# A ConvFFN's down-projection by seven products of half blocks in place of eight, in a two-layer decoder step on one core

## The chip, the core and the metric

The kernel runs on one core of a Trainium2 chip. The metric is the device time of one launch in microseconds (us). The core has a matrix engine (TensorE, PE in the profile; PEld is its loading of weights), a vector engine (VectorE, DVE), a scalar engine (ScalarE, ACT), GpSimd (POOL) and SyncE (SP), which here issues nearly all DMA. Each engine executes its own instructions in order; between engines, semaphores decide.

## What is computed

Two decoder layers over 1024 prompt tokens and 8 x 8 sample tokens, 1088 columns in all (`T`), in float32. Each layer has attention and a gated mixer, and then a gated ConvFFN with 1024 model and 2816 hidden channels:

```python
def _layer(x, c, pos, attend, conv_prev, p):
    ...
    x = x + g_a * (jnp.concatenate([a_out, s_out], axis=-1) @ p['w_out'])
    h = _rmsnorm(x, p['g_ffn']) * (1 + sc_f) + sh_f
    hu = h @ p['w_ffn_in']
    ext = jnp.concatenate([conv_prev.astype(hu.dtype), hu], axis=1)
    conv = p['conv_b'] + sum(p['conv_w'][j] * ext[:, j:j + t] for j in range(CONV_W))
    gate, up = jnp.split(conv, 2, axis=-1)
    x = x + g_f * ((jax.nn.silu(gate) * up) @ p['w_ffn_out'])
    return x, k, v, vg, ext[:, -(CONV_W - 1):]
```

The last product, `silu(gate) * up` by `w_ffn_out` (2816 x 1024), is the down-projection. The scales and shifts (`sh`, `sc`, `g`) come from a conditioning vector by a product with `w_ada`. Outputs are the activations, the key and convolution caches and the gate rows.

## The kernel before

Activations lie transposed: 128 channels on the partitions, the 1088 columns along a row. Every factor of a matmul is split by `split` into a high part (ACT copies it into a shorter float type) and a low part (DVE subtracts that from the original), and a product is three matmuls: high by high, high by low, low by high (`mm3`, lines 304 to 306 of the profile).

A layer runs through these stages, each with its pools of SBUF and PSUM:

- Attention, mixer and output projection. Between its pieces stand calls of `ada`, each 4 matmuls of a 256-column piece of `w_ada`, which make the scales that later stages need; layer 0 has 32 of them left to do, layer 1 has 48.
- **First phase**, the up-projection with convolution and gate. It loops over 22 blocks `f` of 128 hidden channels for the gate and 128 for the up half. The product of the weights by `h` is cut into blocks (two halves of channels by two halves of 544 columns, `HT`) and done by seven products in place of eight, with sums of weights (`diff`, 128x512 on DVE) and of activations. Its matmuls are `prod` (line 918) into the accumulators X, Y, Z, of 272 columns (`HC`) each. PE works through f while DVE and ACT do the convolution of f before (`conv`, lines 949 to 956) and the gate (`gate`, line 960); the result is written to DRAM as `pd[f]` by a DMA of POOL. `tail` closes the last f.
- **Second phase**, the down-projection. `down(g)` runs for six groups: three thirds of the columns (384, 384, 320) by two halves `mh` of the 1024 outputs. A group has four accumulators `y` of one PSUM bank, and loops over all 22 f: `half_unit` loads a 128x512 piece of weights (`ro`) and splits it into `oh` and `ol`, `load_prod` loads a third of `pd[f]` (`pr`) and splits it into `ph` (for the first half only, it is kept for the second), and then come 12 matmuls. The weights are thus loaded and split three times. After a group, `residual` adds its outputs to `xs`, and they go to DRAM. In layer 0 `hook` puts the next layer's norm of a third (squares on ACT, sums on POOL and PE in `nrma`, broadcast by PE in `nrba`, products on DVE) into the groups 2 and 4, and 16 calls of `ada` into the groups 1 and 3. The norm of the last third, and after it the next layer's first products `zv` in `zv_all`, follow the down-projection.

The order of work on an engine is set by the program's scheduler from the order of the code and the free buffers of the pools.

## Time and profile before

| | |
|---|---|
| runs | 2318.65, 2320.19, 2322.41 us; median 2320.19 |
| profiled execution | 2321.23 us, span 2319.4 us |
| busy share | PE 97%, PEld 92%, DVE 67%, ACT 47%, POOL 12% |
| chain that ended last | PE 89%, DVE 5%, DMA 2%, ACT 2%, issue 1%, POOL 1% |
| layer 0: first phase, down-projection | 431.45 to 901.3, 904.28 to 1191.6 us |
| layer 1: first phase, down-projection | 1577.9 to 2044.4, 2051.68 to 2315.1 us |

The span runs from the first to the last instruction; the execution's own time is 1.8 us longer. The chain is followed back from the last instruction to what released each step. The clock granted to PE is 1.00 at full speed. PE's matmuls overlap, so that the spacing of their starts, or their count in a stretch, tells their price and not the length of one. What stands behind "<-" in brackets names what ended an engine's idle time.

### The profile page before, as it was taken

The numbers are of one execution on the slowest core, as the hardware profiler recorded it, in microseconds if no ns is written. First come the engines' busy times: TensorE is split into PE (matmuls) and PEld (weight loads), VectorE is DVE, ScalarE is ACT, GpSimd is POOL, SyncE is SP. The second block draws the span as 40 slices with busy tenths as digits, with TensorE's granted clock in tenths as the row PEclk, the third lists the DMA queues.
The fourth block names the chain that finished last, engine by engine and source line by source line (L and its number), as shares of the span: only waits on it lengthen the run. The fifth ranks groups of instructions, "written<-read, shape, count | busy, mean of one in ns | idle before, by whom it ended". The sixth has DMA issues, their size and how long they took to land.

```text
span 2319.4 us, 41013 instructions
## 1 busy us (share of the span) xinstructions
PE 2258.1 (97%) x15838; PEld 2129.6 (92%) x15838; DVE 1559.5 (67%) x3400; ACT 1087.7 (47%) x2110; POOL 286.5 (12%) x426
## 2 busy tenths in 40 slices
PE   7999999999999999999999999999999999989999
PEld 5898789899999999999988987898999999989999
DVE  5837854887777776464758378369777777764544
ACT  5524533644545445353544255246544544453443
POOL 1000002132111211000000000112211121100000
PEclk9999999999999999999999999999999999999999
DMA  9220244322222224767651002641222222156665
GB/s 354 100 91 1 68 154 161 132 87 77 81 80 79 78 73 155 245 207 236 204 179 61 32 1 77 236 166 47 83 80 77 83 79 78 63 188 196 222 208 169
DMA packets 138116, 289.02 MB, mean 125 GB/s; under 512 B 22400, under 2 KB 63680, under 8 KB 137920
## 3 DMA queue, kind: packets, MB, share of 16 engines
q1 hardware_dynamic: 130176, 261.08, 34.4%
q0 software_dynamic: 7744, 25.33, 2.8%
q8 instruction: 124, 2.03, 0.4%
q14 instruction: 72, 0.59, 0.1%
HBM read 242.54 MB, written 43.80 MB: 123 GB/s over the span
## 4 chain that ended last, share of the span: by engine, by line
PE 89%; DVE 5%; DMA 2%; ACT 2%; issue 1%; POOL 1%; SPq 0%; DVEq 0%; ACTq 0%; POOLq 0%
PE X L918 22%; PE Y L918 11%; PE o L313 7%; PE y L304 7%; PE y L305 7%; PE y L306 7%; PE Z L918 6%; PE zu L313 4%; PE s L644 2%; PE ada L130 1%; PE av L732 1%; PE zv L306 1%; PE q L304 1%; PE zv L305 1%; PE zv L304 1%; PE q L305 1%
## 5 line engine op out<-in xcount | busy, mean ns | idle before, releaser
L304 PE MATMUL y<-ph,oh 128*128 128x384 f32 (+1 forms) x1056 | 347.4, 330 | 10.8 <-ACT ph L181 10.8
L305 PE MATMUL y<-ph,oh 128*128 128x384 f32 (+1 forms) x1056 | 347.0, 329 | 2.4 <-DVE ph L182 2.4
L306 PE MATMUL y<-ph,ol 128*128 128x384 f32 (+1 forms) x1056 | 346.0, 328 | 0.0
L182 DVE TENSOR_TENSOR ol<-ro,oh 128x512 fp32r<-128x512 f32 x264 | 183.1, 698 | 189.5 <-ACT oh L181 172.7
L181 ACT ACTIVATE oh<-ro 128x512 fp32r<-128x512 f32 x264 | 165.5, 628 | 216.9 <-PE y L305 106.2
L951 DVE SCALAR_TENSOR_TENSOR cv<-hu,lc,cv 128x1023 f32<-128x1023 f32 (+1 forms) x168 | 215.1, 1280 | 59.1 <-ACT cv L949 59.1
L304 PEld LDWEIGHTS y<-ph,oh 128*128 128x128 f32 x1056 | 199.2, 189 | 18.1 <-ACT ph L181 11.5
L305 PEld LDWEIGHTS y<-ph,oh 128*128 128x128 f32 x1056 | 199.9, 189 | 3.7 <-DVE ph L182 3.7
L306 PEld LDWEIGHTS y<-ph,ol 128*128 128x128 f32 x1056 | 199.8, 189 | 0.0
L941 POOL COPY hus<-halo 128x16 f32<-128x16 f32 x88 | 85.2, 969 | 366.6 <-issue 258.8
L313 PE MATMUL o<-hhm,wh 128*128 128x384 f32 (+1 forms) x384 | 120.8, 334 | 0.0
L313 PE MATMUL o<-hhm,wl 128*128 128x384 f32 (+1 forms) x384 | 119.1, 329 | 0.3 <-DVE wl L164 0.3
L313 PE MATMUL o<-hlm,wh 128*128 128x384 f32 (+1 forms) x384 | 118.7, 329 | 0.4 <-DVE hlm L182 0.4
L949 ACT ACTIVATE cv<-hu,lc 128x1088 f32<-128x1088 f32 x84 | 108.5, 1291 | 19.3 <-DVE hu L1017 19.3
L182 DVE TENSOR_TENSOR ph<-pr,ph 128x384 fp32r<-128x384 f32 (+1 forms) x132 | 72.2, 551 | 50.9 <-ACT ph L181 50.1
L181 ACT ACTIVATE ph<-pr 128x384 fp32r<-128x384 f32 (+1 forms) x132 | 66.1, 503 | 70.6 <-DMA pr<-pd 68.9
L163 ACT ACTIVATE wh<-r 128x1024 fp32r<-128x1024 f32 x44 | 46.3, 1056 | 91.5 <-PE zu L313 64.8
L164 DVE TENSOR_TENSOR wl<-r,wh 128x1024 fp32r<-128x1024 f32 x40 | 48.9, 1223 | 55.6 <-ACT wh L163 45.7
L313 PEld LDWEIGHTS o<-hhm,wh 128*128 128x128 f32 x384 | 71.7, 189 | 6.6 <-issue 4.9
L956 ACT ACTIVATE cv<-cv 128x1088 f32<-128x1088 f32 x42 | 46.8, 1114 | 64.8 <-DVE cv L953 64.8
L313 PEld LDWEIGHTS o<-hhm,wl 128*128 128x128 f32 x384 | 71.7, 189 | 2.2 <-issue 1.6
L313 PEld LDWEIGHTS o<-hlm,wh 128*128 128x128 f32 x384 | 71.8, 189 | 2.1 <-DVE hlm L182 1.0
(400 smaller groups left out, 6258.9 us busy)
## 6 DMA issues: line engine op xcount, KB each, us to landing
r<-in_w SPq DMA_DIRECT2D x132, 512.0 KB, 3.5
ro<-in_w SPq DMA_DIRECT2D x264, 256.0 KB, 3.3
ra<-in_w_ada SPq DMA_DIRECT2D x64, 512.0 KB, 4.7
pd<-cv POOLq DMA_DIRECT2D x42, 544.0 KB, 3.0
pr<-pd SPq DMA_DIRECT2D x88, 192.0 KB, 3.6
rb<-in_w_ada SPq DMA_DIRECT2D x16, 512.0 KB, 7.7
ra<-in_w_ada SPq DMA_DIRECT2D x32, 256.0 KB, 4.2
pr<-pd SPq DMA_DIRECT2D x44, 160.0 KB, 3.6
```

The lines of the kernel that those rows point to most:

```text
L164: eng.tensor_tensor(out=wl, in0=raw, in1=wh.bitcast(F32), op=ALU.subtract)
L181: r = nc.scalar.activation(out=h, in_=x, func=AF.Copy)
L182: eng.tensor_tensor(out=lo, in0=x, in1=h.bitcast(F32), op=ALU.subtract)
L304: r = nc.tensor.matmul(pt, lhsT=lh, rhs=rh, start=first, stop=False)
L305: nc.tensor.matmul(pt, lhsT=lh, rhs=rl, start=False, stop=False)
L306: nc.tensor.matmul(pt, lhsT=ll, rhs=rh, start=False, stop=last)
L313: nc.tensor.matmul(pts[t][:, :n], lhsT=lhsT, rhs=r[t][:, k, :], start=f, stop=e)
L918: nc.tensor.matmul(pt[:, i, :HC], lhsT=a[:, k * P:(k + 1) * P], rhs=b[:, k, i * HC:(i + 1) * HC], start=(first and k == 0 and a is wh and ...
L941: nc.gpsimd.tensor_copy(rs[:, :, :2], halos[f][:, i])
L949: nc.scalar.activation(out=a, in_=hu, func=AF.Identity, scale=w2, bias=cb)
L951: nc.vector.scalar_tensor_tensor(out=a[:, sh:NP], in0=hu[:, :NP - sh], scalar=wt, in1=a[:, sh:NP], op0=ALU.mult, op1=ALU.add)
L956: nc.scalar.activation(out=a, in_=a, func=AF.Silu)
```

## The change

The product of the second phase is done as the first phase's is. With the weights cut into halves of hidden channels (blocks i and i + 11 of the 22) by halves of outputs, and the activations into the same halves of hidden channels by halves of columns (544), the eight products of half blocks become seven, some of sums of blocks:

- The sums of activations are formed in the first phase: f now runs in pairs (i and i + 11, list `F`), and after each second one `gate` does four additions or subtractions of 128x544 on DVE (the last in `last_sum`, after the next product), and four DMAs write seven blocks, `pd[i]`, of 544 columns, where two wrote two whole ones.
- The sums of weights are formed in the second phase by DVE, 128x512 each: `t1`, `t4` (both kept in SBUF for a later product), `t2` and `t3`.
- Products follow in the order A11, A12, S2, S3, A22, S1 and S4, each of 11 steps i with 4 accumulators of two PSUM banks and 24 matmuls of 272 columns (`mm_pairs`, line 1149 after). S4 is run in two halves of the outputs. Between products DVE adds the accumulators to kept sums (`plus`), ACT copies those of the first (`r1`), and `res_early` and `res_late` add finished quarters to `xs`. The pool "pc" has four tiles of two banks; that leaves no bank free.
- Loads: weights come in as 128x1024, 128x512 or 128x256 pieces, activations as 128x544.
- The next layer's norm: the last third inside the second half of S4, the other two after it. `zv_all` takes the tokens of the last third first.
- The 16 calls of `ada` in layer 0's second phase move: to the attention of both layers and, two of them, ahead of layer 0's first phase.

```diff
     def zv_all(l, st_, h):
-        for j in range(NT):
+        order = [6, 7, 8, 0, 1, 2, 3, 4, 5]
+        for i, j in enumerate(order):
             zv_tile(l, j, st_, h)
...
-            if l == 0 and g > 0:
-                ada(0, 2)
+            if g > 0:
+                ada(l, 4 if l == 0 else (2, 3, 3)[g - 1])
...
-        ada(l, 8)
         if l == 0:
+            ada(1, 16)
+        else:
             ada(1, 8)
...
+        F = [p // 2 + NF // 2 * (p % 2) for p in range(NF)]
...
         def gate(f):
             g, u = cvs.pop((f, 0)), cvs.pop((f, 1))
-            nc.vector.tensor_tensor(out=u, in0=g, in1=u, op=ALU.mult)
-            nc.gpsimd.dma_start(out=pd[f], in_=u)
-            nc.gpsimd.dma_start(out=o_hl[l, f], in_=news.pop(f))
+            r = bp(f"u{l}_{f}") if f == 0 else u
+            nc.vector.tensor_tensor(out=r, in0=g, in1=u, op=ALU.mult)
+            gated[f] = r
+            nc.gpsimd.dma_start(out=o_hl[l, F[f]], in_=news.pop(f))
+            if f % 2 == 0:
+                return
...
+            a, b = gated.pop(f - 1), gated.pop(f)
+            nc.gpsimd.dma_start(out=pd[i][:, 2:4], in_=blocks(b))
+            nc.vector.tensor_tensor(out=a[:, HT:], in0=a[:, HT:], in1=b[:, HT:], op=ALU.add)
+            nc.gpsimd.dma_start(out=pd[i][:, 0:2], in_=blocks(a))
+            c = bp(f"s{l}_{f}")
+            nc.vector.tensor_tensor(out=c[:, :HT], in0=a[:, HT:], in1=a[:, :HT], op=ALU.subtract)
+            nc.vector.tensor_tensor(out=c[:, HT:], in0=b[:, HT:], in1=c[:, :HT], op=ALU.subtract)
+            nc.gpsimd.dma_start(out=pd[i][:, 4:6], in_=blocks(c))
...
-        def down(g, hook):
-            t, mh = divmod(g, 2)
...
+        def w_p1(i):
+            raw = wload([(i, 0, 1024)])
+            nc.vector.tensor_tensor(out=t1[:, i], in0=raw[:, 512:], in1=raw[:, :512], op=ALU.subtract)
+            return wsplit(raw[:, :512])
...
+        def w_p6(i):
+            raw = wload([(NI + i, 512, 1024)])
+            t2 = wtmp()
+            nc.vector.tensor_tensor(out=t2, in0=raw[:, :512], in1=t1[:, i], op=ALU.subtract)
+            nc.vector.tensor_tensor(out=t4[:, i], in0=t4[:, i], in1=t2, op=ALU.subtract)
+            return wsplit(t2)
...
+        def mm_pairs(pts, ms, wt, at, first, stop, col=0):
+            for m in ms:
+                c = slice(m * P - col, m * P - col + P)
+                for a, b in ((0, 0), (0, 1), (1, 0)):
+                    for i in range(2):
+                        mark[0] = nc.tensor.matmul(
+                            pts[m][:, i, :HC], lhsT=wt[a][:, c], rhs=at[:, b, i * HC:(i + 1) * HC],
+                            start=(first and a == 0 and b == 0), stop=(stop and a == 1), skip_group_check=True)
...
+        g1 = quad("g1")
+        block_prod(g1, w_p1, C_A11, True, False)
+        for m in range(4):
+            nc.scalar.activation(out=half(r1[m]), in_=g1[m][:, :, :HC], func=AF.Copy)
+        block_prod(g1, w_p2, C_A12, False, True, load_x4)
+        for m in range(4):
+            res_early(m, g1[m][:, :, :HC])
+        g2 = quad("g2")
+        block_prod(g2, w_p6, C_S2, True, False)
+        for m in range(4):
+            plus(u2[m], g2[m], r1[m])
+        block_prod(g2, w_p7, C_S3, False, False)
+        for m in range(4):
+            plus(u3[m], g2[m], r1[m])
+        block_prod(g2, lambda i: wsplit(t4[:, i]), C_A22, False, True)
+        for m in range(4):
+            plus(r1[m], g2[m], r1[m])
+        for m in range(4):
+            res_late(m, r1[m])
+        g3 = quad("g3")
+        block_prod(g3, lambda i: wsplit(t1[:, i]), C_S1, True, False)
...
+        for mh in range(2):
+            for i in range(NI):
+                wt = wsplit(wload([(NI + i, 512 + 256 * mh, 768 + 256 * mh)])[:, :256])
...
```

Where the instructions of an engine change their order, three places are shown, as tile names stand in the program: a number behind the underscore tells one buffer from the next.

**DVE at the start of layer 1's down-projection**, from the product that ends the gating (`cv1_211`). Before (`ol1`, `ph1` are low parts of weights and activations):

```order
L960 TENSOR_TENSOR cv1_211_23015<-cv1_210_23051,cv1_211_23015 128x1088
L182 TENSOR_TENSOR ol1_000_23096<-ro1_000_23093,oh1_000_23095 128x512
L182 TENSOR_TENSOR ph1_00_23101<-pr1_00_23099,ph1_00_23101 128x384
L182 TENSOR_TENSOR ol1_100_23119<-ro1_100_23116,oh1_100_23118 128x512
L182 TENSOR_TENSOR ph1_10_23124<-pr1_10_23122,ph1_10_23124 128x384
```

After (`s1`, `d1` and the first `cv1` are the sums of activations, `t11` a sum of weights, `ah1` activations):

```order
L971 TENSOR_TENSOR cv1_211_23189<-cv1_210_23225,cv1_211_23189 128x1088
L980 TENSOR_TENSOR cv1_201_22974<-cv1_201_22974,cv1_211_23189 128x544
L983 TENSOR_TENSOR s1_21_23237<-cv1_201_22974 128x544
L984 TENSOR_TENSOR s1_21_23237<-cv1_211_23189,s1_21_23237 128x544
L989 TENSOR_TENSOR d1_23241<-cv1_211_23189,s1_21_23237 128x544
L1117 TENSOR_TENSOR t11_23290<-ro1_23296 128x512
L184 TENSOR_TENSOR ol1_23300<-ro1_23296,oh1_23299 128x512
L184 TENSOR_TENSOR ah1_00_23305<-ar1_23303,ah1_00_23305 128x544
```

Four sums of activations and a sum of weights have come between the gating and the first low parts.

**DVE at the handover from the third product to the fourth** in layer 0, after (`ot0` is `t3`, `g200` to `g203` are the accumulators; before there is no such place):

```order
L1134 TENSOR_TENSOR ot0_11788<-ro0_11785 128x512
L184 TENSOR_TENSOR ol0_11715<-ot0_11712,oh0_11714 128x512
L184 TENSOR_TENSOR ah0_15_11682<-ar0_11680,ah0_15_11682 128x544
L1134 TENSOR_TENSOR ot0_11826<-ro0_11823 128x512
L184 TENSOR_TENSOR ol0_11753<-ot0_11750,oh0_11752 128x512
L1165 TENSOR_TENSOR u200_10406<-g200_11207,r100_10398 128x544
L1165 TENSOR_TENSOR u201_10407<-g201_11208,r101_10399 128x544
L1165 TENSOR_TENSOR u202_10408<-g202_11209,r102_10400 128x544
L1165 TENSOR_TENSOR u203_10409<-g203_11210,r103_10401 128x544
L184 TENSOR_TENSOR ah0_25_11720<-ar0_11718,ah0_25_11720 128x544
L184 TENSOR_TENSOR ah0_35_11758<-ar0_11756,ah0_35_11758 128x544
```

The four additions stand behind the weights of the fourth product's steps 0 to 2 and the activations of its steps 0 and 1, and ahead of the activations of step 2.

**PE behind layer 0's last down-projection matmul.** Before, `nrma12` are the sums of the last third's norm (the last two of six rows), and `zv1` the next layer's first products:

```order
L216 MATMUL nrma12_13489<-cs_63,accn0_10784 64x1
L216 MATMUL nrma12_13489<-cs_63,nsqn027_13451 64x1
L304 MATMUL zv1_0_13598<-wh1_0_13467,hha10_11406 128x512
L304 MATMUL zv1_1_13659<-wh1_0_13467,hha10_11406 128x512
L304 MATMUL zv1_2_13719<-wh1_0_13467,hha10_11406 128x512
```

After, the sums (the last two of six rows) and the broadcast (`nrba10`) of the first third, and the sums of the second (the first two of six rows, behind which `zv1` begins):

```order
L218 MATMUL nrma10_13493<-cs_63,accn0_12425 128x1
L218 MATMUL nrma10_13493<-cs_63,nsqn007_13448 128x1
L241 MATMUL nrba10_13516<-dga10_13517,cs_63 128x128 x3
L218 MATMUL nrma11_13566<-cs_63,accn0_12425 128x1
L218 MATMUL nrma11_13566<-cs_63,nsqn017_13450 128x1
```

The next layer's first product now follows the broadcast of a norm whose sums need the last accumulators; before, it followed the sums alone.

## Rows read from the trace of the kernel before

**Rows 1.** The page: busy time by engine, the chain that ended last

```profile
PE 2258.1 (97%) x15838; PEld 2129.6 (92%) x15838; DVE 1559.5 (67%) x3400; ACT 1087.7 (47%) x2110; POOL 286.5 (12%) x426
...
PE 89%; DVE 5%; DMA 2%; ACT 2%; issue 1%; POOL 1%; SPq 0%; DVEq 0%; ACTq 0%; POOLq 0%
```

**Rows 2.** Stretches: engines' busy us and count, clock, DMA share, GB/s

```profile
core 0: us, PE busy (x) PEld busy (x) DVE busy (x) ACT busy (x) POOL busy (x), PEclk, DMA share, GB/s
...
1720.00:1820.00 100.00, 100.00 (x800) 100.00 (x800) 75.91 (x110) 48.98 (x78) 19.48 (x37) 1.00 0.23 78
2060.00:2140.00 80.00, 80.00 (x463) 80.00 (x462) 40.25 (x66) 34.33 (x62) 0.00 (x0) 1.00 0.68 216
2240.00:2310.00 70.00, 70.00 (x479) 70.00 (x478) 35.90 (x66) 29.27 (x52) 0.00 (x0) 1.00 0.66 208
```

**Rows 3.** Groups by line and shape: busy us, mean ns

```profile
L182 DVE TENSOR_TENSOR ol<-ro,oh 128x512 fp32r<-128x512 f32 x264 | 183.1, 698 | 189.5 <-ACT oh L181 172.7 <-PE ada L130 11.5 <-PE y L306 2.4
...
L1017 DVE TENSOR_TENSOR hu<-Y,r 128x544 f32<-128x544 f32 x42 | 30.4, 724 | 54.4 <-PE Y L918 54.4
...
L182 DVE TENSOR_TENSOR hla<-hfa,hha 128x320 fp32r<-128x320 f32 x8 | 3.7, 486 | 0.1
```

**Rows 4.** Time line, start of layer 1's down-projection: start, length, idle before

```profile
2043.99 0.41 PE L918 MATMUL X<-A22h,T4l 128*128 128x272 f32 x2
...
2050.73 1.29 DVE L960 TENSOR_TENSOR cv<-cv,cv 128x1088 f32<-128x1088 f32 x1 [1.24 <-ACT cv L956]
...
2051.68 1.01 PE L304 MATMUL y<-ph,oh 128*128 128x384 f32 x2 [7.28 <-ACT ph L181]
...
2053.15 0.69 PE L305 MATMUL y<-ph,oh 128*128 128x384 f32 x1 [0.46 <-DVE ph L182]
```

**Rows 5.** Time line, start of layer 0's down-projection

```profile
904.28 0.98 PE L304 MATMUL y<-ph,oh 128*128 128x384 f32 x4 [3.02 <-ACT ph L181]
...
906.88 0.69 PE L305 MATMUL y<-ph,oh 128*128 128x384 f32 x1 [1.62 <-DVE ph L182]
```

**Rows 6.** Stretches after waits of PE

```profile
906.16:912.99 6.83, 6.11 (x19) 6.11 (x20) 4.43 (x9) 2.56 (x4) 0.54 (x1) 0.50 0.63 206
1018.00:1025.00 7.00, 5.83 (x36) 5.51 (x35) 6.68 (x22) 4.20 (x8) 0.00 (x0) 1.00 0.69 224
```

**Rows 7.** Time line, from layer 0 to layer 1

```profile
1191.31 0.31 PE L306 MATMUL y<-ph,ol 128*128 128x320 f32 x1
...
1194.91 0.38 PE L216 MATMUL nrma<-cs,accn 128*128 128x1 f32 x2 [3.29 <-POOL accn L206]
...
1196.21 2.03 PE L304 MATMUL zv<-wh,hha 128*128 128x512 f32 x4
1196.32 0.16 DVE L222 TENSOR_SCALAR msa<-nrma 128x2 f32<-128x2 f32 x1 [2.32 <-PE nrma L216]
...
1199.52 0.80 PE L305 MATMUL zv<-wl,hha 128*128 128x512 f32 x1 [1.27 <-DVE wl L164]
...
1199.76 0.68 DVE L238 TENSOR_SCALAR dga<-cs,rra 128x128 f32<-128x128 f32 x3
```

**Rows 8.** Time line of PE: conditioning matmuls, a broadcast of the norm

```profile
425.40 3.66 PE L130 MATMUL ada<-ra,cact 128*32 128x256 f32 x64
...
961.98 0.64 PE L130 MATMUL ada<-ra,cact 128*32 128x256 f32 x8
...
964.86 0.64 PE L130 MATMUL ada<-ra,cact 128*32 128x256 f32 x8
...
1020.85 0.94 PE L239 MATMUL nrba<-dga,cs 128*128 128x128 f32 x6 [1.17 <-DVE dga L238]
```

**Rows 9.** DMA queue from 904 to 1191: packets, MB, share of 16 engines

```profile
q1 hardware_dynamic: 37981, 61.24, 67.7%
```

**Rows 10.** Time line, end of the program

```profile
2314.75 0.31 PE L306 MATMUL y<-ph,ol 128*128 128x320 f32 x1
...
2316.39 0.22 DVE L300 TENSOR_TENSOR xb1m<-xb1m,resy 128x64 f32<-128x64 f32 x1
```

More of the change, by code (lines that the diff above doesn't have):

```diff
@@ L1021, in hybrid_decoder_kernel @@
             r1 = keep(x_, "r1", f)
+            if f % 2 and late4:
+                late4.pop()()
             ahead("B11")
@@ new lines, in hybrid_decoder_kernel, with wload @@
+        mark = [None, None]
+        last = l + 1 == DEPTH
+        if not last:
+            xd = dp.tile([KD, P, T], F32, tag="xd", name="xd")
+        x_out = y if last else xd
+        def wload(parts, n=1024):
+            raw = pl["wb"].tile([P, 1024], F32, tag="raw", name=f"ro{l}", bufs=3)
+            o = 0
+            for f, a, b in parts:
+                mark[1] = nc.sync.dma_start(out=raw[:, o:o + b - a], in_=w[l, U_FO + f, :, a:b])
+                o += b - a
+            return raw
@@ new lines, in block_prod, with quad, plus @@
+        def block_prod(pts, wf, c, first, stop, hook=None):
+            for i in range(NI):
+                wt = wf(i)
+                at = a_load(i, c)
+                mm_pairs(pts, range(4), wt, at, first and i == 0, stop and i == NI - 1)
+                if hook:
+                    hook(i)
+        def quad(nm):
+            return [pl["pc"].tile([P, 2, 512], F32, tag="c", name=f"{nm}{l}{m}", bufs=4) for m in range(4)]
+        def plus(dst, pt, a):
+            nc.vector.tensor_tensor(out=half(dst), in0=pt[:, :, :HC], in1=half(a), op=ALU.add)
```

197 lines of the change are left out of this document (113 added, 84 removed).

## The prediction, made before the changed kernel had run

> **What bounds the kernel now.** I read the page first, then the span cut into stretches, then the ends of the two down-projections on a time line. The page says TensorE: PE busy 97% of 2319.4 us and 89% of the chain that ended last; DVE is at 67%, ACT at 47%, POOL at 12% [rows 1]. So the time is the number of matmuls times their spacing, plus the places where PE waits. The stretches give the spacing, all at a granted clock of 1.00 [rows 2]. The up-projection, which already has the seven products and 272-column matmuls, issues 800 in 100 us: 125.0 ns each. The down-projection issues 463 of 384 columns in 80 us, 172.8 ns, and 479 of 320 columns in 70 us, 146.1 ns. Per column that is 0.460, 0.450 and 0.457 ns: in this kernel a matmul's price goes by its columns, although each has a weight load of its own (as many PEld as PE in the same rows). The waits of PE around the down-projection are at its two starts [rows 4, 5], at the hand-over from layer 0 to layer 1 [rows 7], at broadcasts of the norm inside it (one of two shown [rows 8]) and at the end [rows 10].
>
> **The matmuls.** Before, a layer's down-projection has 1056 matmuls of 384 and 528 of 320 columns: 1056 x 0.1728 + 528 x 0.1461 = 182.5 + 77.1 = 259.6 us. After it has 7 products x 11 pairs of channels x 4 x 6 = 1848 matmuls of 272 columns; the nearest row, the same shape with the same alternation of high and low parts, gives 1848 x 0.1250 = 231.0 us. That is 28.6 us a layer, **-57.2 us** for both. An eighth of 259.6 would be 32.5; four pieces of 272 columns cost more than three of 384, 384 and 320.
>
> Here a rule of the Trainium skill speaks against the change. The section "Back-to-back issue gap" of "TensorE: Matmul & The Clock Gate" says that the spacing in a stream is set by the weight load and the matmul together, with 81 ns at 128 columns and 131 ns at 512. Between these, an estimate in a straight line gives 114, 106 and 100 ns for 384, 320 and 272 columns, and the sum over both layers would be 353 us before and 368 after: 15 us lost. Rows 2 disagree (172.8, 146.1 and 125.0 ns), so I go by the rows.
>
> **Starts of the down-projection.** PE restarts when DVE has the low part of the first activations. In layer 1 the last matmul of the first phase starts at 2043.99, the product that ends the gating starts at 2050.73 and takes 1.29, and the low part of the activations lets PE go on at 2053.15 [rows 4]. After, DVE's order puts four sums of 128x544 behind that product (0.72 each by the row of 724 ns), then one sum of weights and one low part of weights (0.70 each) and the low part of the activations (0.72) [rows 3]: 2050.73 + 1.29 + 2.88 + 1.40 + 0.72 = 2057.0, 3.9 later. Matmuls after such a wait run at the lower clock: 19 in 6.83 us, where 39.5 would fit, 3.6 us lost [rows 6]. That loss was there before, and I add 1.3 for a later recovery: **+5.2** (2 to 8). In layer 0 the low part was released at 906.88 [rows 5]; after, a sum and a low part of weights stand ahead of it, 1.4 us, while the four sums come later: **+1.5** (0 to 4).
>
> **Sums of activations in the first phase.** Two channels f take four additions more, 4 x 0.72 = 2.9 us of DVE per 42.1 us of PE (168 matmuls per f). DVE is at 75.9 us of 100 there [rows 2] and goes to about 83. PE has no wait in these rows, and after the change DVE still idles some 17 us of 100. I take **+0.5**; if DVE's order makes PE wait 0.5 us at each of 42 f, 21.
>
> **Sums of weights and the splits in the second phase.** A step i is 24 matmuls, 3.0 us of PE. DVE has in it at most two sums and two low parts, 2.8 us (the third product, S2), else 1.4 to 2.1; ACT has two copies to the high parts, and was busy 43% of the stage before [rows 2]. DVE's order prepares two steps ahead, so this hides behind PE, but in the third product DVE has only 0.2 us a step to spare and four residuals of 0.7 on top: 11 x 2.8 + 2.9 = 33.7 against PE's 33.0, in both layers. I take **+1** (0 to 6, if 0.3 us a step are lost).
>
> **Handovers between products.** The four accumulators now fill all of PSUM (two banks each), so a product starts only when DVE or ACT has read the last one out. DVE's order has the four additions behind the splits for two steps of the next product, and PE's order within a step is by accumulator: the first is finished 2.25 us before the last. An addition takes 0.72, about the 0.75 us in which PE works through one accumulator, so PE stays ahead by little. I take 0.25 us for each of 12 handovers, **+3**; from 0 to 2.9 (four additions) plus 3.6 (lost at the lower clock) each.
>
> **Second half of the seventh product, layer 0.** The norm of the last third now runs inside these 11 steps of 12 matmuls (16.5 us of PE). I add up DVE's order: two additions and two residuals 2.9, eleven small operations and three diagonals 2.9, eight products with the norm and eight low parts at 0.49 [rows 3], 7.8, sixteen 64-column ones at 0.22 [rows 10], 3.5, the low parts of weights some 4: 21 us. PE waits for the diagonal (about 1.5; at 1020.85 the wait for one was 1.17 [rows 8]) and for the low parts of weights queued behind the norm on DVE: **+4** (0 to 8).
>
> **From layer 0 to layer 1.** Before, PE's last matmul starts at 1191.31, the norm's sums at 1194.91 and the next layer's matmuls at 1196.21, with one more gap of 1.27 at 1199.52 [rows 7]; the broadcast is then long covered. After, two thirds of the norm are still to do, and their broadcast stands ahead of the next layer's first matmul in PE's order: additions, residuals and squares 2.1 + 1.6, norm sums 1.3 as before, small operations 2.2 (1196.32 to 1199.76 less 1.2 for a split of weights in between), diagonals 0.7, broadcast 0.7, second sums 1.3, so 9.9 us against 4.9 + 1.3, and 0.5 for weights behind three products with the norm. The two broadcasts inside the down-projection, at 1.2 each [rows 8], go: **+2.8** net, with 1.0 for the last broadcast (0 to 8).
>
> **Conditioning matmuls moved.** Sixteen calls leave layer 0's down-projection, where each made a block of 12 matmuls 2.88 us in place of 2.07 (from one at 961.98 to the next at 964.86) [rows 8]: -12.8. They go to the attention of both layers and the gap before the first phase, at 0.46 each (64 matmuls, eight to a call, in 3.66 us [rows 8]) to 0.8: +7.4 to +12.8. Calls that filled the wait for the norm before now come behind it. **-1.5** (-5.4 to +3).
>
> **Transfers.** The stage moved 61.24 MB at 67.7% of the engines in 287 us [rows 9], so 315 GB/s at 100%. After, the first and the fourth product want 802 KB per 3.0 us (267 GB/s), the second, with eight loads of x, 323 GB/s over its 33 us. Rows are longer than before (4 KB for 2 and 1.5), and loads run three to four ahead: **+1** (0 to 10). **End:** an addition more, and a later output: **+0.7**, as from the last matmul at 2314.75 to 2319.4 it is 4.7 now [rows 10].
>
> **Sum.** -57.2 + 5.2 + 1.5 + 0.5 + 1 + 3 + 4 + 2.8 - 1.5 + 1 + 0.7 = -39.0 us. The profiled execution took 2321.2 (span 2319.4), 1.0 above the median of the runs: 2321.2 - 39.0 = **2282 us**.
>
> **Rivals.**
> A, slower: *the handover*. With no spare bank, DVE reaches the four additions late (each split queued ahead of them on it costs 0.7), PE waits for all of them and restarts at the lower clock: 2.9 + 3.6 = 6.5 us at each of 12, 78 in place of the 3 in the sum: 2357. It ends slower than before from (39 + 3) / 12 = 3.5 us a handover. For it: no bank is free, and the granted clock was 0.50, the lower of its two levels of 1.2 and 2.4 GHz, after the wait of 3.02 us [rows 5, 6]. Against: after one of 1.17 us it stayed at 1.00 [rows 6, 8], DVE is half idle in the stage, and its order has the additions in place. 4%.
> B, *a price per weight load*: PEld is busy without a break at every width [rows 2], and the pairs of load and matmul go from 3168 to 3696. Were a 272-column pair to cost in this stage what a 320-column one does, 3696 x 0.1461 = 540 against 519: +21 in place of -57, 2360. The rule of the Trainium skill cited above is of this kind. Against: the 800 in 100 us are just such pairs. 1%.
> C, *late transfers or a slowed first phase*: +10 or +21 more: 2292 to 2303. For it: 323 GB/s is above the 315 of the stage, and DVE at 83% has little slack. 17%.
> D, *the losses are smaller*: no wait in the third and the seventh product or at a handover, and starts at their lower bounds, 1 + 4 + 3 + 3.2 + 1.5 us: 2269. 15%.
> That the matmuls are not fewer is excluded by the order of instructions; only their spacing is open.
>
> **Chances.** My own case, 2273 to 2291, has 58%; C 17%, D 15% (some of it below 2264), A 4%, B 1%; 5% for several losses together that end between 2303 and 2345. The range 2264 to 2303 leaves out some 15%. Within 0.2% of before (4.6 us, about what a measurement of this kernel can tell from no change) 3%; slower 5%; faster 92%.
>
> **What would show it.** Right: 24 matmuls per 3.0 us all through the down-projection, about 251 us in layer 0 and 242 in layer 1 from its first matmul to its last (287.0 and 263.1 before [rows 4, 5, 7, 10]); PE's wait at layer 1's start ended by DVE near 13 us after the last matmul; small waits at handovers. Wrong: the clock under 1 at product boundaries (A), a spacing above 0.13 us (B), PE waiting on DMA in the second product or f-periods above 21.1 us in the first phase (C).

## The result, and the profile after

The changed kernel takes 2285.61 us (median of four runs, 2283.77 to 2287.43), beside 2319.61 for the kernel before on the same chip: a ratio of 0.9851, 95% interval 0.9834 to 0.9869. Forecast were 2282 us, 2264 to 2303. The profiled execution of after took 2283.77 us with a span of 2282.0, against 2321.23 and 2319.4: 37.4 us of span gone in these two executions, and 34.0 us by the medians, where the sum had 39.0.

The page of after, busy time by engine, and the chain that ended last (the lines of [rows 1]):

```profile
PE 2202.3 (97%) x16366; PEld 2075.8 (91%) x16366; DVE 1654.8 (73%) x3534; ACT 1057.2 (46%) x2052; POOL 321.9 (14%) x470
...
PE 84%; DVE 7%; DMA 3%; ACT 2%; issue 1%; POOL 1%; SPq 0%; DVEq 0%; ACTq 0%; POOLq 0%
```

PE is still the bound; DVE has gained 95 us of work and 2 points of the chain. Stretches of after (columns as in [rows 2]): first phase, two whole products of layer 0 (S2, then S3), and layer 1's down-projection:

```profile
1720.00:1820.00 100.00, 100.00 (x800) 100.00 (x799) 80.77 (x117) 50.71 (x78) 22.12 (x42) 1.00 0.29 94
...
985.07:1018.22 33.15, 33.15 (x267) 33.15 (x266) 26.73 (x43) 12.99 (x23) 0.00 (x0) 1.00 0.86 282
1018.22:1051.36 33.14, 33.14 (x266) 33.14 (x265) 20.14 (x32) 12.98 (x23) 0.00 (x0) 1.00 0.47 139
...
2090.00:2190.00 100.00, 100.00 (x799) 100.00 (x798) 68.32 (x106) 38.96 (x66) 0.00 (x0) 1.00 0.66 206
```

The 272-column matmul costs 100 / 799 = 125 ns in its new place too. From the first matmul of a product to the first of the next pass 33.15 us in the products 2 to 6 of both layers: 264 spacings of 0.1254 and 0.05 over. First to last, a down-projection takes 249.1 us in layer 0 (912.03 to 1161.09; 251 forecast) and 240.1 in layer 1 (2036.44 to 2276.49; 242 forecast).

The start in layer 1, time line of after (answers to [rows 4]):

```profile
2028.61 0.41 PE L925 MATMUL X<-A22h,T4l 128*128 128x272 f32 x2
...
2035.36 1.29 DVE L971 TENSOR_TENSOR cv<-cv,cv 128x1088 f32<-128x1088 f32 x1 [1.24 <-ACT cv L963]
...
2036.44 1.05 PE L1149 MATMUL g<-ah,oh 128*128 128x272 f32 x3 [7.42 <-ACT ah L183]
2036.68 0.72 DVE L980 TENSOR_TENSOR cv<-cv,cv 128x544 f32<-128x544 f32 x1
...
2039.48 0.68 DVE L1117 TENSOR_TENSOR t<-ro 128x512 f32<-128x512 f32 x1
2040.08 0.69 DVE L184 TENSOR_TENSOR ol<-ro,oh 128x512 fp32r<-128x512 f32 x1
...
2040.68 0.72 DVE L184 TENSOR_TENSOR ah<-ar,ah 128x544 fp32r<-128x544 f32 x1
...
2041.45 0.82 PE L1149 MATMUL g<-ah,oh 128*128 128x272 f32 x2 [3.97 <-DVE ah L184]
```

This is the queue that the prediction wrote out: product, four sums, a sum of weights, two low parts, and PE released by DVE 12.7 us after the last first-phase matmul (2028.74; forecast 13).

The seventh product in layer 0 (1117.65 to 1161.09; its second half begins at 1138.5), PE, DVE, POOL and ACT of after:

```profile
1129.57 0.52 PE L1149 MATMUL g<-ah,oh 128*128 128x272 f32 x2 [0.89 <-ACT ah L183]
1130.79 0.52 PE L1149 MATMUL g<-ah,oh 128*128 128x272 f32 x2 [0.70 <-DVE ah L184]
...
1147.91 0.85 PE L241 MATMUL nrba<-dga,cs 128*128 128x128 f32 x6 [2.41 <-DVE dga L240]
...
1125.57 1.54 DVE L184 TENSOR_TENSOR ah<-ar,ah 128x544 fp32r<-128x544 f32 x1
...
1124.39 7.21 POOL L208 TENSOR_TENSOR accn<-accn,nsqn 128x320 f32<-128x320 f32 x6 [0.79 <-ACT nsqn L204]
...
1128.00 0.53 ACT L204 ACTIVATE nsqn<-xb0m 128x384 f32<-128x384 f32 x1 [0.92 <-POOL accn L208]
```

The first two rows lie in the product's first half already. An `ah` that takes 0.72 us elsewhere takes 1.54 here, beside the additions of squares on POOL, and a square on ACT (`nsqn`), behind which splits for PE stand, waits 0.92 us for POOL. Twice in this product the granted clock is 0.50, the lower level, with 15 and 17 matmuls where 27 would fit (columns as in [rows 2]):

```profile
1131.63:1135.04 3.41, 3.24 (x15) 2.92 (x14) 3.41 (x6) 1.53 (x4) 1.12 (x1) 0.50 0.31 101
1148.69:1152.11 3.42, 3.42 (x17) 3.42 (x17) 3.24 (x12) 2.81 (x7) 0.00 (x0) 0.50 0.11 38
```

From layer 0 to layer 1, after (answers to [rows 7]):

```profile
1160.96 0.41 PE L1149 MATMUL g<-ah,ol 128*128 128x272 f32 x2
...
1164.57 0.38 PE L218 MATMUL nrma<-cs,accn 128*128 128x1 f32 x2 [3.20 <-POOL accn L208]
...
1169.08 1.62 PE L241 MATMUL nrba<-dga,cs 128*128 128x128 f32 x6 [2.84 <-DVE dga L240]
...
1172.91 1.63 PE L306 MATMUL zv<-wh,hha 128*128 128x512 f32 x3
...
1197.94 0.92 ACT L183 ACTIVATE hha<-hfa 128x384 fp32r<-128x384 f32 x2
1198.88 1.28 ACT L359 ACT_TABLE_LOAD   x1
...
1200.18 2.07 ACT L359 ACTIVATE gz<-zv 128x512 f32<-128x512 f32 x4
...
1200.83 0.80 PE L306 MATMUL zv<-wh,hha 128*128 128x512 f32 x1 [3.73 <-ACT gz L359]
```

And the stretches behind the two waits:

```profile
1165.76:1176.00 10.24, 7.40 (x28) 6.71 (x29) 7.89 (x24) 5.73 (x10) 0.00 (x0) 0.50 0.39 137
1199.89:1206.72 6.83, 5.89 (x14) 4.64 (x15) 6.41 (x52) 3.44 (x8) 0.00 (x0) 0.50 0.00 1
```

The first `zv` matmul comes 11.8 us after the last of the down-projection (4.9 before). A second hole, which the prediction doesn't have, opens at 1197.1: PE waits 3.73 us for `gz`, which stands on ACT behind the norm of the second third (`hha`) and a table load, and goes on at the lower clock.

### The profile page after: what moved, and what is told of

Read it like the earlier page. It is cut to its first block, busy times and chain, and to the rows that moved or that the text cites. A ratio compares the mean times of both kernels' runs of the same rounds, so it can differ in the third digit from the quotient of the medians.

```text
span 2282.0 us, 41942 instructions
## 1 busy us (share of the span) xinstructions
PE 2202.3 (97%) x16366; PEld 2075.8 (91%) x16366; DVE 1654.8 (73%) x3534; ACT 1057.2 (46%) x2052; POOL 321.9 (14%) x470
## 4 chain that ended last, share of the span: by engine, by line
PE 84%; DVE 7%; DMA 3%; ACT 2%; issue 1%; POOL 1%; SPq 0%; DVEq 0%; ACTq 0%; POOLq 0%
PE X L925 21%; PE g L1149 18%; PE Y L925 11%; PE o L315 8%; PE Z L925 5%; PE zu L315 4%; PE s L647 2%; PE av L735 1%; PE ada L132 1%; PE q L306 1%; PE zv L306 1%; PE q L307 1%; PE q L308 1%; PE zv L308 1%; PE zv L307 1%
## 5 line engine op out<-in xcount | busy, mean ns | idle before, releaser
L1149 PE MATMUL g<-ah,oh 128*128 128x272 f32 x2464 | 418.5, 291 | 21.6 <-ACT ah L183 12.6
L1149 PEld LDWEIGHTS g<-ah,oh 128*128 128x128 f32 x2464 | 353.5, 190 | 24.4 <-ACT ah L183 13.7
L1149 PE MATMUL g<-ah,ol 128*128 128x272 f32 x1232 | 257.0, 290 | 0.0
L1149 PEld LDWEIGHTS g<-ah,ol 128*128 128x128 f32 x1232 | 195.2, 191 | 0.1
L956 ACT ACTIVATE cv<-hu,lc 128x1088 f32<-128x1088 f32 x84 | 108.5, 1292 | 37.4 <-DVE hu L1046 37.2
L184 DVE TENSOR_TENSOR ah<-ar,ah 128x544 fp32r<-128x544 f32 x154 | 113.0, 738 | 12.2 <-ACT ah L183 10.4
L183 ACT ACTIVATE ah<-ar 128x544 fp32r<-128x544 f32 x154 | 99.5, 647 | 15.2 <-DMA ar<-pd 12.3
L184 DVE TENSOR_TENSOR ol<-t,oh 128x512 fp32r<-128x512 f32 x66 | 45.6, 691 | 78.9 <-ACT oh L183 78.9
L183 ACT ACTIVATE oh<-t 128x512 fp32r<-128x512 f32 x66 | 41.6, 631 | 106.8 <-PE g L1149 106.7
L971 DVE TENSOR_TENSOR cv<-cv,cv 128x1088 f32<-128x1088 f32 x42 | 54.3, 1293 | 27.0 <-ACT cv L963 27.0
L166 POOL TENSOR_TENSOR wl<-r,wh 128x1024 fp32r<-128x1024 f32 x4 | 9.6, 2407 | 453.9 <-DMA cwh<-in_cache_k 238.8
```

The source lines that it names most:

```text
L166: eng.tensor_tensor(out=wl, in0=raw, in1=wh.bitcast(F32), op=ALU.subtract)
L183: r = nc.scalar.activation(out=h, in_=x, func=AF.Copy)
L184: eng.tensor_tensor(out=lo, in0=x, in1=h.bitcast(F32), op=ALU.subtract)
L956: nc.scalar.activation(out=a, in_=hu, func=AF.Identity, scale=w2, bias=cb)
L971: nc.vector.tensor_tensor(out=r, in0=g, in1=u, op=ALU.mult)
L1149: mark[0] = nc.tensor.matmul(pts[m][:, i, :HC], lhsT=wt[a][:, c], rhs=at[:, b, i * HC:(i + 1) * HC], start=(first and a == 0 and b == 0), ...
```

## The experiments

All times are medians, ratios are to the kernel before on the same chip, with 95% intervals. Excess of a product is its time over 264 spacings of 0.12536 us (the seventh's time ends at its last start). A thousandth of the ratio is 2.3 us; the changed kernel's own interval is 0.9834 to 0.9869, so a gain of a few us shows in the trace of its place and not in the ratio alone.

**e1_ada: the kernel before with the moved conditioning calls alone.**

```diff
-            if l == 0 and g > 0:
-                ada(0, 2)
+            if g > 0:
+                ada(l, 4 if l == 0 else (2, 3, 3)[g - 1])
...
-                if g in (1, 3) and 1 <= f <= 8:
-                    ada(1, 1)
```

> The kernel before with one part of the change alone: the 16 calls of ada leave layer 0's down-projection for the attention of both layers and the gap before layer 0's first phase. Theory (a call costs PE 0.8 us beside the down-projection and 0.46 to 0.8 where it goes): layer 0's down-projection 12.8 us shorter, 287.0 to 274.2 from its first to its last matmul; the way to layer 0's first phase about 8 longer and the attention of layer 1 about 3, as in the changed kernel; in sum -1.5 to -2 us, 2317. Rival (in the down-projection they cost more than the spacing shows, since the splits wait for them): -5 us or more, 2314.

2316.82 us against 2317.03, 0.9999 (0.9989 to 1.0008). In the trace layer 0's down-projection is 16.5 us shorter (270.6 for 287.0), the first phase of layer 0 starts 9.3 later, the transition is 1.4 and layer 1's gate products 2.8 us longer. By the medians the move is even (-0.2 us, interval -2.5 to +1.9): the calls cost as much in their new places.

**e6_margin: sixteen more additions a layer, at four handovers.** Each addition of an accumulator is done twice (the second result is used by nothing), so that the next product's first matmuls are released later.

```diff
+            if again:
+                nc.vector.tensor_tensor(out=half(px), in0=pt[:, :, :HC], in1=half(a), op=ALU.add)
```

> The changed kernel with one more addition of 128x544 on DVE ahead of each of the 16 additions at the 4 handovers from the third product on (32 more in all, their results unused): the cost of a handover for DVE is doubled, 5.8 us for 2.9. Theory of the prediction (PE keeps ahead by little, since an addition takes 0.72 and PE takes 0.75 for an accumulator): PE now waits 0.7 us for the third and the fourth accumulator, 1.4 us at each of 8 handovers, 11 us, 2297. The slower rival of the prediction (a wait brings the lower clock with it): 1.4 + 1.7 to 3.6 each, 25 to 40 us, 2310 to 2325. A second rival (additions start as each accumulator ends, and two prepared steps leave room for all): no wait, 2286.

2301.89 us, 0.9932 (0.9915 to 0.9948). Three of the four doubled handovers cost next to nothing: the products 4 to 6 have an excess of 0.32, 0.63 and 0.54 in layer 0 and 0.32, 0.63 and 0.88 in layer 1, of which 0.3 comes from a spacing that is 1% wider in the down-projections of this run (product 2, without such a handover ahead, has 0.34), so 0.5 us at most a handover. The stretch with the third-to-fourth handover stays at full clock, without a gap:

```profile
1016.50:1049.90 33.40, 33.40 (x266) 33.40 (x265) 23.12 (x37) 13.10 (x22) 0.00 (x0) 1.00 0.53 165
```

Behind the fourth, the seventh product does lose: excess 13.7 and 4.1 for 10.3 and 1.1. In layer 1 PE waits only 0.32 us at the handover itself, but DVE comes later to the residuals and the splits behind them, the next load of weights goes out 8.1 us after the product's start (5.8 in the changed kernel), and PE waits for ACT's split of what it brings:

```profile
2268.24 0.42 ACT L183 ACTIVATE oh<-ro 128x256 fp32r<-128x256 f32 x1 [7.87 <-DMA ro<-in_w]
...
2269.82 0.39 PE L1149 MATMUL g<-ah,oh 128*128 128x272 f32 x1 [2.05 <-ACT ah L183]
```

The rest lies for the most part at layer 1's start (18.5 for 14.6 lost), where the extra buffer moved the first load. So the handover has a margin of some 2.5 us at three of four places, about 3 us were lost behind the fourth, and rival A was far from its turning point.

**e9_sums2: the first phase with its sums formed twice** (four more subtractions of 128x256 a pair, unused).

```diff
+            e = bp(f"e{l}_{f}")
+            for h in range(2):
+                for s in (a, b):
+                    nc.vector.tensor_tensor(out=e[:, h * HT:h * HT + HT], in0=s[:, HT:], in1=s[:, :HT], op=ALU.subtract)
```

> The changed kernel with four more subtractions of 128x256 for each of the 16 pairs of first-phase blocks, whose result nothing reads, so that the first phase forms the sums twice over. By the changed kernel's trace one such subtraction takes about 0.43 us alone, so 1.7 us more a pair and 27 us over both layers, in a phase in which VectorE is busy some 85 per cent. Theory (the sums of the first phase cost nothing because VectorE still has room there): VectorE's share rises to about 90 per cent and both first phases keep their 468 to 469 us within 2 us each; time 2284 to 2291, with the waits at layer 1's start a microsecond or so longer, since the last pair's additions stand there. Rival (the room is already used up, and any further addition comes late for the products): each pair's 1.7 us shows, both first phases grow by 10 to 14 us, time 2300 to 2315.

(The expectation has the size wrong: `HT` is 544 columns and a layer has 11 pairs, so the work added is not 27 but 2 x 11 x 4 x 0.72 = 63 us, which makes the test a harder one.) 2290.14 us, 0.9885 (0.9872 to 0.9899). DVE in layer 0's first phase, first after, then e9:

```profile
460.00:880.00 420.00, 418.10 (x3332) 417.47 (x3331) 348.38 (x512) 213.89 (x330) 110.37 (x176) 1.00 0.29 94
```

```profile
460.00:880.00 420.00, 417.66 (x3316) 417.06 (x3315) 367.91 (x548) 213.62 (x330) 108.85 (x176) 1.00 0.28 94
```

DVE goes from 83% to 88%, and the phases take 470.8 and 467.5 us for 468.9 and 467.6. The 1.9 us in layer 0 are no more than scatter: runs that leave its first phase as it is take 468.6 to 470.9 (e2 470.9, e3 470.6). What is lost is at the starts (2.9 and 2.4 us more), where the last pair's sums stand ahead of the low parts. The rival, and with it the half of C that spoke of a slowed first phase, falls.

**e2_squares: the squares of the first half moved ahead of the seventh product.**

```diff
-                if mh == 0 and not last and i < 4:
-                    for t in range(2):
-                        square_sum(acc, xs[i], t, i, f"n{l}")
...
+        block_prod(g3, lambda i: wsplit(t1[:, i]), C_S1, True, False, squares)
```

> Of the changed kernel, the 8 squares of the first four blocks of x (thirds 0 and 1), with the 8 steps on POOL that follow them, are moved from the first half of the seventh product of layer 0 into the steps 4 to 7 of the sixth. Theory (ACT's splits stand behind squares that wait for POOL, whose additions take 1.2 us each): the stall of PE at 1128.4 to 1133.5 us goes, with the half clock that follows it; the seventh product of layer 0 has 43.4 us now and should have about 39.5, and the kernel 2285.6 - 4 = about 2282 us. Rival (the splits are late because DVE is still busy with four additions and the residuals, 7 us from 1117.1 on): the same stall stays, 43 us, and the time is 2285.6. The sixth product stays at 33.15 us by both, if ACT has room for 0.5 us a step more.

2286.34 us, 0.9858 (0.9843 to 0.9872); the seventh product's excess is 10.15 for 10.33, its waits only stand elsewhere (1.54 us on DVE's `u` at 1120.03, which stands behind a split for which ACT waits 2.30 us on a load). Three of POOL's nine additions are left in the first half. So it isn't enough to move the squares: another wait takes their place.

**e10_stores: stores of finished quarters issued by POOL in place of SP.**

```diff
-            nc.sync.dma_start(out=x_out[m, :, HT:], in_=xs[m][:, HT:])
+            nc.gpsimd.dma_start(out=x_out[m, :, HT:], in_=xs[m][:, HT:])
```

> Of the changed kernel, the stores of the second half of the columns of x (8 a layer, after the fifth and the sixth product) are issued by POOL in place of SP. Theory (SP's queue is held from 1116.3 to 1124.7 us by four stores that wait for DVE; the loads of the seventh product's steps stand behind them, land 3.5 us later and let PE wait at 1128.4): layer 0's seventh product falls from 43.4 us by 3 to 5, layer 1's from 34.2 to 33.1; about 2281 us. Rival (POOL's additions slow DVE, which the stores don't change): layer 0's seventh product stays within 1 us of 43.4, 2285.

2289.65 us, 0.9879 (0.9864 to 0.9894): worse in the very product, excess 15.1. The first load of weights behind the stores now goes out 6.7 us after the product's start, for 7.1, so SP's queue had held it by 0.4 us at most. What made it worse stands on DVE and POOL:

```profile
1122.37 7.58 DVE L184 TENSOR_TENSOR ol<-ro,oh 128x256 fp32r<-128x256 f32 x1
...
1123.90 5.76 POOL L208 TENSOR_TENSOR accn<-accn,nsqn 128x384 f32<-128x384 f32 x6
...
1130.64 0.59 PE L1149 MATMUL g<-ah,oh 128*128 128x272 f32 x1 [5.59 <-DVE ah L184]
```

Six additions run back to back on POOL, 0.96 us each, and one low part on DVE, which takes 0.42 us elsewhere, lasts 7.58 us, until they are through. PE waits for the `ah` behind it. So the run says little of SP's queue beyond the 0.4 us, and shows the rival's mechanism at its largest.

**e8_dve: layer 0's running sums of squares on DVE in place of POOL.**

```diff
-                        square_sum(acc, xs[i], t, i, f"n{l}")
+                        square_sum(acc, xs[i], t, i, f"n{l}", nc.vector)
```

> Of the changed kernel, the running sums of squares for the next layer's norm that POOL does in layer 0's second phase (additions of 128x384 and 128x320, 1.2 us each while DVE works too) are done by DVE (about 0.55 us). Theory (DVE's subtractions of 0.72 us take up to 1.54 while POOL adds, and ACT's squares wait for POOL; so PE's splits are late in the seventh product): layer 0's seventh product falls from 43.4 us by 3 to 5, and the norm's sums after the last matmul come about 0.5 sooner, so about 2281 us. Rival (the loads of the seventh product are late since they stand on SP behind four stores of x that wait for DVE): 43 us as before, 2286, or more, by DVE's 5 us of further work.

2280.36 us, 0.9839 (0.9825 to 0.9854); the seventh product's excess falls from 10.33 to 7.55. Groups of DVE from 1100 to 1160 (columns as in [rows 3]), after:

```profile
L184 DVE TENSOR_TENSOR ah<-ar,ah 128x544 fp32r<-128x544 f32 x14 | 12.1, 870 | 3.2 <-ACT ah L183 2.8
L184 DVE TENSOR_TENSOR ol<-ro,oh 128x256 fp32r<-128x256 f32 x22 | 10.6, 487 | 4.6 <-ACT oh L183 4.6
...
L178 DVE SCALAR_TENSOR_TENSOR rtna<-rtna,msa 128x3 f32<-128x3 f32 x3 | 1.3, 417 | 0.1
```

and with the sums on DVE:

```profile
L184 DVE TENSOR_TENSOR ah<-ar,ah 128x544 fp32r<-128x544 f32 x14 | 10.1, 724 | 4.0 <-ACT ah L183 3.6
L184 DVE TENSOR_TENSOR ol<-ro,oh 128x256 fp32r<-128x256 f32 x22 | 9.0, 419 | 2.4 <-ACT oh L183 2.4
L208 DVE TENSOR_TENSOR accn<-accn,nsqn 128x384 f32<-128x384 f32 x10 | 4.9, 552 | 0.0
...
L178 DVE SCALAR_TENSOR_TENSOR rtna<-rtna,msa 128x3 f32<-128x3 f32 x3 | 0.5, 161 | 0.1
```

DVE does 13 additions more (ten shown), 6.4 us, and what it did before gets faster by about as much. Operations with both inputs in SBUF lose their excess (870 to 724 ns, 487 to 419, 417 to 161). ACT's squares no longer wait for POOL either, so the run takes two things away at once. The ratio is lower by 0.0012, 2.8 us, which the intervals don't tell from nothing, but the traces agree: with the sums on DVE (e8, e12, e14b) the seventh product's first half takes 18.0 to 18.2 us, in the changed kernel, e2, e3, e4, e5, e9 and e13b 20.2 to 21.1. So some 2.7 us of it came from POOL's additions, by one way or the other. The next layer's first product doesn't come sooner, as was expected: 12.4 us after the last matmul, for 11.8.

**e4_pool: the last pair's four sums on POOL.**

```diff
+            eng = nc.vector if f < NF - 1 else nc.gpsimd
-            nc.vector.tensor_tensor(out=a[:, HT:], in0=a[:, HT:], in1=b[:, HT:], op=ALU.add)
+            eng.tensor_tensor(out=a[:, HT:], in0=a[:, HT:], in1=b[:, HT:], op=ALU.add)
```

> Of the changed kernel, the four sums of activations of the last pair of channels are done by POOL in place of DVE, in both layers. Theory (in layer 1 four sums of 0.72 us stand on DVE between the gating and the low parts for which PE waits): from the last matmul of the first phase PE loses 2.9 us less at the start of layer 1's down-projection, 11.7 in place of 14.6 over the first 140 matmuls, and some 0.7 less in layer 0, where one sum stands ahead of the second step; the kernel takes about 2282 us. Rival (the low clock after the wait decides: its length is set by the wait that is left, 5 us for 7.4): 4 to 5 us less in layer 1. Second rival (POOL and DVE hinder each other on SBUF, so that DVE's subtractions of 0.69 to 0.72 us grow by over a third while POOL adds): less than 1.5 us gained.

2284.68 us, 0.9852 (0.9838 to 0.9867). Layer 1 loses 12.2 us at its start for 14.6, so the sums did stand in PE's way; layer 0 loses 0.3 and its second product 1.7 us more, and the total doesn't move. DVE, POOL and PE there:

```profile
2040.94 1.86 DVE L184 TENSOR_TENSOR ah<-ar,ah 128x544 fp32r<-128x544 f32 x1
...
2040.77 1.44 POOL L981 TENSOR_TENSOR cv<-cv,cv 128x544 f32<-128x544 f32 x1
...
2042.85 0.82 PE L1150 MATMUL g<-ah,oh 128*128 128x272 f32 x2 [2.20 <-DVE ah L184]
```

**e5_t1late: the sum of weights after the low part of the activations.**

```diff
-            nc.vector.tensor_tensor(out=t1[:, i], in0=raw[:, 512:], in1=raw[:, :512], op=ALU.subtract)
+        def sum_t1(i):
+            raw = raws1.pop(i)
+            after(nc.vector.tensor_tensor(out=t1[:, i], in0=raw[:, 512:], in1=raw[:, :512], op=ALU.subtract), lows[0])
```

> Of the changed kernel, the sum of weights t1 of each step of the first product is issued on DVE behind the low part of that step's activations, not ahead of it. Theory (in layer 0 the sum waits 1.1 us for a DMA that still reads the memory it writes to, and then takes 0.7, ahead of the low part for which PE waits): the loss at layer 0's start falls from 10.25 us by 1.8 to about 8.4, in layer 1 by 0.7 from 14.55 to 13.9; the kernel takes about 2283 us. Rival (the same DMA holds up the next instructions as well, and PE only waits later, at the second step): less than 0.5 us in layer 0, 2285.

2290.03 us, 0.9877 (0.9862 to 0.9892); the intervals overlap, but in the trace layer 0's down-projection takes 257.1 us for 249.1. Layer 0's first step gets shorter (7.54 for 8.37 us), but its first product has an excess of 11.0 for 6.8: the loaded weights are held until their sum is formed, the next load starts late, and ACT waits 7.89 us for it at 929.67. The order of DVE here decides when transfers start.

**e3_bank: two `zv` accumulators in other banks of PSUM.**

```diff
-        pt = bank("mm", f"zv{l}_{j}")
+        pt = bank("at" if l and j in (1, 2) else "mm", f"zv{l}_{j}")
```

> Of the changed kernel, two of the nine accumulators of the next layer's first products (token blocks 1 and 2) come from the other four PSUM banks. Theory (at 1196.7 us PE waits 3.7 us for a bank that is freed by the activation gz, which stands on ACT behind the norm of the second third and a table load of 1.3 us): the wait of 3.7 us and the half clock from 1199.9 to 1206.7 go, 3.7 + 3.4 = 7 us, so the next layer's first products end 7 us sooner and the kernel takes about 2278.5 us. Rival (the wait only moves: products that would run instead need the second third's norm, which is as late, or the wait comes back two blocks later at the next bank): 0 to 2 us gained, 2284 to 2285.6.

2285.98 us, 0.9854 (0.9838 to 0.987): the same. The wait for `gz` is still 3.73 us, at 1204.31, and ahead of the 97th `zv` matmul as in the changed kernel. It isn't those two accumulators; what `gz` frees there no run shows.

**e13b_fill: eight of layer 1's conditioning calls ahead of that place.**

```diff
             zv_tile(l, j, st_, h)
+            if l and i == 2:
+                ada(l, 8)
```

> The changed kernel with layer 1's eight modulation steps that stand between its own gate products moved into the transition, ahead of the first zv tile that waits for gz. Theory (the 3.73 us that TensorE waits there for ScalarE's gz, and the slow clock of 6.83 us that follows, are a hole that any ready work fills): the wait falls below 1.5 us, the slow stretch behind it goes, the stretch of layer 1's gate products gets about 2.8 us shorter, and the transition stays within 2 us of its 75.4; time 2277 to 2282. Rival (the steps only push the tiles behind them back, since their own weights or broadcasts come late there): the gate products get shorter by 2.8 and the transition longer by as much or more; time 2284 to 2289.

2277.77 us, 0.9828 (0.9815 to 0.9842). The same stretch of the transition, after and then e13b:

```profile
1192.50:1207.00 14.50, 10.77 (x36) 8.35 (x35) 12.43 (x64) 11.10 (x22) 0.00 (x0) 0.76 0.26 87
```

```profile
1192.50:1207.00 14.50, 14.50 (x108) 9.01 (x106) 12.07 (x59) 11.58 (x21) 0.00 (x0) 1.00 0.66 235
```

The hole is gone and the clock stays up. The transition keeps its length (75.8 us for 75.4) with the eight calls in it, and layer 1's gate products, up to the first matmul behind them, take 50.8 us for 54.2. By the trace's span the gain is 4.6 us, by the ratios 0.0023 or 5.3 us, with intervals that overlap a little.

**e12_best and e14b_best: e8 and e4 together, and these with e13b.**

> The changed kernel with two edits together: the running sums of squares in layer 0's second phase on VectorE (alone 2280.4 us), and the four sums of each layer's last first-phase pair on GpSimd (alone 2284.7 us). Theory (they act at two places that have nothing in common): the gains add, 2.7 us in the last product of layer 0 and its transition and about 2 us at layer 1's start, time 2277 to 2281. Rival (GpSimd's sums at the end of layer 0's first phase slow VectorE's own there, as its squares did in the second, and eat their gain): 2280 to 2284, with layer 0's first down products over 2 us longer than in the changed kernel.

> The run before this one's two edits and the eight modulation steps of layer 1 in the transition ahead of the tile that waits for gz, all three together. Theory (three holes at three places): about 3 to 5 us below the kernel with two edits, 2272 to 2277. Rival (the third only moves the wait): the same as with two, within 2 us.

2278.81 us, 0.9833 (0.982 to 0.9846), and 2276.23 us, 0.9819 (0.9805 to 0.9832). In e12 layer 1 loses 12.1 us at its start and layer 0's seventh product has an excess of 5.9; layer 0's second product loses 1.2 us, so both readings of the pair are partly right, and with e8 alone at 0.9839 the second edit can't be told from nothing. With all three edits the kernel is the fastest of those run, ahead of the changed kernel by 0.0032 of the time, 7.4 us; the third edit's 2.6 us on top of e12 lie inside the intervals.

## Why the prediction was right

The time came out 3.6 us above 2282, and its direction and its main term held. Three terms missed by 6 to 7 us each: the seventh product and the transition cost more, and the norm's leaving the groups gave back more. That they partly cancelled is in part luck. Measured from the two traces (us):

| term | predicted | measured |
|---|---|---|
| matmuls | -57.2 | -57.6 |
| starts, layer 1 and layer 0 | +5.2, +1.5 | +4.4, +2.3 |
| sums in the first phase | +0.5 | +0.7 |
| third product; handovers | +1; +3 | 0; +0.6 |
| seventh product: second half in layer 0 | +4 | +6.0 |
| seventh product: first half in layer 0; layer 1 | none | +4.3; +1.1 |
| transition | +5.2 | +11.1 |
| norm gone from the groups 2 and 4 | -2.4 | -8.6 |
| conditioning calls moved | -1.5 | -2.8 |
| transfers; end | +1; +0.7 | 0; +0.8 |
| sum | -39.0 | -37.7, for -37.4 |

The terms are each from one execution. That before was 1.6 us above its median and that after 1.8 below, so 3.4 of the 37.4 us are scatter between executions, and no term is known better than to 2 us or so.

- **Matmuls.** Groups of before in which nothing else runs took 45.76 us for 264 matmuls of 384 columns and 38.71 for 264 of 320 (layer 1), 520.9 us in all; after, 2 x 1848 x 0.12536 = 463.3 us. The step "a price goes by its columns" held, and B, a price per weight load, fell. The rule of the Trainium skill weighed there (section "Back-to-back issue gap" of "TensorE: Matmul & The Clock Gate") would have lost 15 us; 799 in 100 us decide against it.
- **Starts.** Loss is the time from the last first-phase matmul to the 140th of the down-projection, over its spacings: 10.14 to 14.55 us in layer 1, 7.94 to 10.25 in layer 0. The queue on DVE was right row by row; e4 shows that taking the four sums out of it gives 2.4 us back.
- **First phase.** From the first to the last matmul 468.9 and 467.6 us, for 469.5 and 466.3. DVE's idle share covered the sums, as e9 shows with twice as many.
- **Handovers, rival A.** 0.05 us each for 0.25. The prediction counted an addition against PE's work on one accumulator and expected splits queued ahead to make it late; e6 shows that even eight additions in the place of four cost 0.5 us at most at three of the four handovers tried, and some 3 us behind the one into the seventh product.
- **Seventh product.** The excess is 10.3 us in layer 0 and 1.1 in layer 1. The prediction had a term for the second half in layer 0 alone; there 6.0 us were lost, inside its 0 to 8. The wait for the diagonal was 2.41 us, for 1.5. Low parts queued behind the norm, the term's other part, let PE wait nowhere there; in their place stand what the sum left out, the matmuls of the norm itself (1.2 us for its sums, 0.8 for the broadcast) and the lower clock behind the wait (some 1.6). What failed is that the first half, in both layers, was put at nothing without a reason: 20.85 us in layer 0 and 17.8 in layer 1, for 132 spacings or 16.55. In layer 0 squares stand among ACT's splits there, and POOL's additions slow both ACT and DVE; e8 gives 2.7 us back in this half and 0.1 in the other. The 1.6 us that it leaves are near the 1.2 of layer 1, where ACT waits 4.76 us for a load of weights at 2250.40; what makes this load late no run takes apart.
- **Transition.** To the first `zv`, 11.8 us for 9.9 forecast, with the granted clock at 0.50 from 1165.76 to 1176, under which the broadcast takes 1.62 us. From the first `zv` to the last it is 63.6 us for 59.4, 4.2 more where the sum had 0.2. This is the wait for `gz` with the lower clock behind it, less the gap and the lower clock that stood there before: the prediction asked what ends the wait for the norm, not what stands next on ACT when two thirds of the norm come after the down-projection. That order is read from the rows of ACT, and no run changes it; e13b shows that the hole can be filled.
- **Norm removed from the groups.** Here the step counted the wait for a broadcast alone, 1.2 us each [rows 8]. The groups 2 and 4 of layer 0 took 49.23 us from 1007.25 and 43.86 from 1108.87 to the starts of the next groups, where layer 1's, without a norm, took 45.76 and 38.71: 8.6 us, all gone. The matmuls of the norm themselves and what came behind the wait had been left out, as in the seventh product, where they go. In the trace of e1, with the calls alone gone, group 4 takes 41.19 us for 43.86, so 2.7 of the 8.6 can as well be put to the calls ahead of it.
- **Conditioning calls.** The groups 1 and 3 took 52.41 and 52.39 us in layer 0 and 45.76 each in layer 1, so 13.3 us go, and 10.5 come back before layer 0's first phase (8.1) and, less 0.4, among layer 1's gate products (2.8). e1 by its medians has -0.2 us, -2.5 to +1.9, so the -2.8 lies at the edge of what it allows; layer 0's first phase also starts anywhere from 437.4 to 440.9 us in runs that change nothing ahead of it.
- **Transfers, the rest of C.** No wait of PE in the second to sixth product, and 328 GB/s were moved in layer 0's second. (The 323 of the prediction should have been 315: eleven steps of 541 KB and eight loads of x of 557 KB in 33 us, so that point for C was weaker than it said.) Loads did come late in e5, where a buffer held them, and in the seventh product.

## What to carry to other kernels

Here an eighth of the matmuls was traded for additions on a vector engine that had idle time in every step. Inside the products this paid nearly in full (57.6 us won, 0.05 lost at a handover); some 30 us were lost again at the seams: starts, the last product, the way to the next layer, and 11 won by what left the stream. At a seam, write out the queue of every engine up to the first product that runs freely, not just of the one that ends the first wait; and when a step is removed from a stream, price it by the stretch that contained it, less its matmuls, rather than by its visible wait. A hole at a seam can be closed with ready work that is owed anyway, as in e13b. And a forecast whose terms miss by 6 us each way can still land within 4: compare the terms, not the sum.

## What the hardware showed beyond the expectation

DVE's operations on two SBUF inputs get slower while POOL runs an addition of its own: 128x544 takes 0.72 us alone, 1.54 beside the sums of squares and 1.86 beside a sum of POOL's (e4), 128x256 on average 487 ns for 419, and one of three columns 417 ns for 161. Beside six additions in an unbroken row, one of 128x256 took 7.58 us (e10), while the additions kept to 0.96 us each. An operation that reads one of its two large inputs from PSUM keeps its time: in the kernel before, a residual of 128x384 (`y` lies in PSUM) takes 0.61 us beside an addition of POOL's, and 0.61 on average alone:

```profile
1007.79 1.02 POOL L206 TENSOR_TENSOR accn<-accn,nsqn 128x384 f32<-128x384 f32 x1 [48.93 <-ACT nsqn L202]
...
1008.05 0.61 DVE L293 SCALAR_TENSOR_TENSOR xb0m<-y,mod,xb0m 128x384 f32<-128x384 f32 x1
```

The Trainium skill says in "SBUF — State Buffer", section "Who interferes with whom", that a vector instruction with two SBUF inputs contends with a GpSimd instruction that reads SBUF, and one with a single such input doesn't. The traces agree with both, and give the sizes. So work moved to an idle POOL isn't free for DVE, and in e8 the seventh product got 2.8 us shorter when DVE did the additions as well.
